# A weight ring laid out in steps of 32 bytes beside the activations: one core, a two-layer decoder trunk

## The chip, the core and the metric

The kernel runs on one core of a Trainium2 chip. The metric is device time in microseconds (us) of one execution. The kernel before takes 1014.76 us (median of 3 runs, 1014.67 to 1014.93). The profile shown here was taken of the run of 1014.67 us; its instructions span 1012.9 us, and the remaining 1.8 us lie before the first and behind the last of them.

The engines are named as the profile names them: PE (TensorE, matmul), PEld (its weight loads, which run beside the matmuls), DVE (VectorE), ACT (ScalarE), POOL (GpSimd), SP (SyncE, which issues the DMAs).

## What is computed

The reference is a trunk of two layers on 256 rows of 1024 numbers. Each layer is a SwiGLU block, a token mixer and a second SwiGLU block, each with RMSNorm before and behind it:

```python
def swiglu(h, w_gate, w_up, w_down):
    return (jax.nn.silu(h @ w_gate) * (h @ w_up)) @ w_down

for layer in range(DEPTH):
    g = norm_gains[layer]
    h = rmsnorm(x, g[0])
    x = x + 0.5 * rmsnorm(swiglu(h, w_ffn_gate[layer, 0], w_ffn_up[layer, 0], w_ffn_down[layer, 0]), g[1])
    h = rmsnorm(x, g[2])
    x = x + rmsnorm(token_mixer(h, w_in[layer], w_out[layer], ...), g[3])
    h = rmsnorm(x, g[4])
    x = x + 0.5 * rmsnorm(swiglu(h, w_ffn_gate[layer, 1], ...), g[5])
```

Everything is float32. The hidden width of a SwiGLU block is 2816 and the mixer's input projection is 3072 wide, so nearly all the arithmetic is dense products of 256 rows with 1024-deep weights.

## The kernel before

**Three matmuls per product.** A float32 operand is split into a high part (rounded to fp32r) and a low part (the rest). `mm3` forms one product as high by high, high by low and low by high, so each 128-deep step of a product is three matmuls, each with its own weight load of 128 columns.

**The weight ring.** All weights pass through `half`: SP issues a DMA of 512 KB into one of 5 `raw` buffers, ACT copies it to the high part of a ring buffer (line 271), and DVE writes the low part (line 274). There are 10 ring buffers, `ring0` to `ring9`, each of two parts (high and low) of 1024 floats per partition. PE reads them from there, and a buffer is given back when its last matmul is through.

**The activations.** `xt` (two parts, 8 x 256 floats) holds the normed input of the current block, transposed. The 12 `h` buffers (512 floats) hold, in pairs of high and low, the hidden rows of a SwiGLU block, the mixed heads of the mixer, and its values.

**Which operand moves.** A matmul loads one operand (128 columns, the weight load) and streams the other (the moving operand). The program has three large kinds, all recorded at line 362, and the profile names them with the moving operand first:
- `xt,ring`, 256 columns, 4320 of them: the ring is loaded, `xt` moves. These are the gate and up products (`gb`) and the mixer's queries and keys (`qk`). In `gb`, 96 matmuls follow one another and use four ring buffers, 24 each; a gate or up tile lies in two buffers, and PE changes between them every 12 matmuls.
- `ring,xt`, 256 columns, 1056: `xt` is loaded and the ring moves. These are the first gate and up tiles of each block (`ga`) and the mixer's values (`vstep`).
- `ring,h`, 512 columns, 1248: `h` is loaded and the ring moves. These are the down products (`down`, 24 or 12 in a row, two ring buffers) and the mixer's output.

**Order.** `Program.run` plans all operations at build time, by their listed durations, and writes each engine's instructions in that order. The plan does not know where a buffer lies.

**Where the buffers lie.** `Slots.take` makes the tile of a slot when the slot is first used, and the pool lays the tiles one behind the other in that order, each rounded up to 32 bytes. So the place of a buffer modulo 256 bytes follows from the small tiles that happened to be made before it. In the built program `xt` (both parts), `ring0` and `ring1` lie at 96 modulo 256, `ring2` to `ring9` and `h1` to `h11` at 160, and `h0` at 32. The two parts of a ring buffer lie at the same place modulo 256. All slices that matmuls read begin at multiples of 512 bytes within their buffers, so the place modulo 256 of an operand is that of its buffer.

Of the kernel before, what the change touches and what calls it, by code (L numbers as in the profile page):

```python
# [8 lines left out]
F32 = mybir.dt.float32  # L9
# [5 lines left out]
SEQ, D, FF, DEPTH = 256, 1024, 2816, 2  # L15
KC = D // 128
# [14 lines left out]
RING = 10  # L31
# [34 lines left out]
    return c  # L66


class Slots:


    def __init__(self, pool, tag, n, shape, parts=1):
        self.pool, self.tag, self.shape, self.parts = pool, tag, shape, parts
        self.idle = list(range(n))
        self.n = 0

    def take(self, dtype):
        i = self.idle.pop(0)
        self.n += 1
        t = [self.pool.tile(self.shape, dtype, tag=f"{self.tag}{i}_{p}", name=f"{self.tag}{i}_{p}_{self.n}") for p in range(self.parts)]  # L80
        return i, (t[0] if self.parts == 1 else t)


# [15 lines left out]
class Program:  # L99
# [7 lines left out]
    def op(self, eng, dur, fn, after=(), bufs=(), spare=None, lag=None):  # L107
        o = Op()
        o.eng, o.dur, o.fn, o.after, o.bufs = eng, dur, fn, [a for a in after if a is not None], list(bufs)
        o.spare, o.lag, o.idx = spare or {}, lag, len(self.ops)  # L110
        for b in o.bufs:
            b.left += 1
        self.ops.append(o)
        return o
# [99 lines left out]
def act_us(n, psum, extra=0):  # L214
    return (0.05 if psum else 0.092) + 0.000833 * n + 0.093 * extra
# [6 lines left out]
def trunk(tc, x, norm_gains, w_gate, w_up, w_down, w_in, w_out, dlam, subln, consts, out):  # L222
    nc = tc.nc
    ctx = ExitStack()
    P1 = ctx.enter_context(tc.tile_pool(name="one", bufs=1))
# [3 lines left out]
    G = Program()  # L229
    op = G.op  # L230
    PS = Slots(PSM, "ps", 8, [128, 512])
    RAW = Slots(P1, "raw", NRAW, [128, 1024])
    RNG = Slots(P1, "ring", RING, [128, 1024], 2)
    XTS = Slots(P1, "xt", 1, [128, KC, SEQ], 2)
    H2 = Slots(P1, "h2", 12, [128, 512])
    ES = Slots(P1, "e", N_ES, [128, 512])
    PT = Slots(P1, "pt", N_PT, [128, 512])
    SN = Slots(P1, "sn", N_SN, [128, 384])
# [18 lines left out]
    def half(pieces, cut=2):  # L257

        h = Half()
        raw, h.ring = Buf(RAW), Buf(RNG, F32R)  # L260

# [76 lines left out]
    def warm():  # L338

        z, p = Buf(H2, BF16), Buf(PS)  # L340
        o = op("POOL", 0.2, lambda: nc.gpsimd.memset(z.t, 0.0), [], [z])
# [19 lines left out]
    def mm(o, a, b, start=False, stop=False):  # L361
        nc.tensor.matmul(o, a, b, start=start, stop=stop, skip_group_check=True)  # L362
# [12 lines left out]
    def first_gain(i):  # L375

        p = Buf(PS)
        o = op("PE", 1.0, lambda: mm(p.t, ones, grow[:, HALF[i]], True, True), [o_row, o_small], [p])
# [79 lines left out]
    class XT:  # L458


        def __init__(self):
            self.b = Buf(XTS, F32R)
            self.done = [None, None]
# [7 lines left out]
    def turn(T, xt, hs):  # L471
        xt.done[T] = []
        for b in range(2):
            h, oh = hs[b]
            p = Buf(PS)

# [23 lines left out]
    def rows_op(p, c0, xt, T, hs, first):  # L500

        o = None
        for kh in range(2):
            def pe(kh=kh):
                for k in range(4 * kh, 4 * kh + 4):
                    wh, wl = wk(hs, k)
                    mm3(p.t[:, c0:c0 + 256], xt.hi(k, TS(T)), xt.lo(k, TS(T)), wh, wl, first and k == 0, k == KC - 1)
            o = op("PE", 1.31, pe, [xt.done[T][kh], o] + hs[kh].ready, [p, xt.b, hs[kh].ring])
        return o


    def ffn(l, s, xt, na, turn1, g, final, nxt, pre):
# [4 lines left out]
        def tile_(kind, j):  # L517
            if (kind, j) not in tiles:
                if kind == "D":
                    tiles[kind, j] = [half_row(wd, 256 * j + 128 * c) for c in range(2)]  # L520
                else:
                    tiles[kind, j] = half_cols(wg if kind == "G" else wu, 256 * j)
            return tiles[kind, j]
# [3 lines left out]
        def hbuf(j):  # L527
            if j not in hb:
                hb[j] = (Buf(H2, F32R), Buf(H2, F32R))
            return hb[j]  # L530
# [4 lines left out]
        def ga(j, T):  # L535
            pg, pu, sg = Buf(PS), Buf(PS), Buf(ES)
            og = rows_op(pg, 0, xt, T, tile_("G", j), True)
            a = op("ACT", act_us(256, True), lambda: nc.scalar.activation(sg.t[:, :256], pg.t[:, :256], AF.Silu), [og], [pg, sg])
            ou = rows_op(pu, 0, xt, T, tile_("U", j), True)
            m = op("DVE", dve_us(256), lambda: nc.vector.tensor_tensor(sg.t[:, 256:], pu.t[:, :256], sg.t[:, :256], OP.mult), [ou, a], [pu, sg])  # L540
            rows[j, T] = (sg, m)

        def hturn(j, T):
            sg, m = rows[j, T]
            p = Buf(PS)
            bh, bl = hbuf(j)
# [14 lines left out]
        def gb(j):  # L561
# [3 lines left out]
            for part in range(2):  # L565
                p = Buf(PS)
                hs = tile_("GU"[part], j)
# [75 lines left out]
    def mixer(l, xt, turn1, g, nxt, o_cst, o_misc):  # L643
# [5 lines left out]
        def vstep(T, t):  # L649
            if vt[t] is None:  # L650
                vt[t] = half_v(wi, t)
            if t % 2 == 0:
                V[T, t // 2] = (Buf(PS), Buf(H2), [])
            p, v, os = V[T, t // 2]
# [128 lines left out]
        def put_mixed(i, src, after, buf):  # L783
            t = Buf(H2, F32R)
            o1 = op("ACT", act_us(256, True), lambda: nc.scalar.activation(t.t[:, 0:256], src(), AF.Copy), after, [buf, t])
            o2 = op("DVE", dve_us(256), lambda: nc.vector.tensor_tensor(t.t[:, 256:512], src(), t.t[:, 0:256].bitcast(F32), OP.subtract), [o1], [buf, t])
            mixed[i] = (t, o2)
# [186 lines left out]
    xt = XT()  # L974
# [99 lines left out]
```

## Time and profile before

| | before |
|---|---|
| median of 3 runs | 1014.76 us |
| profiled execution | 1014.67 us, span 1012.9 us |
| granted TensorE clock, mean | 0.998 of 2.4 GHz |
| PE busy | 997.9 us, 99% |
| PEld busy | 923.8 us, 91% |
| DVE busy | 632.1 us, 62% |
| ACT busy | 582.3 us, 57% |
| DMA | 182.86 MB, mean 181 GB/s |

A matmul's row shows the length of one instruction from its start to its modelled end, 276 to 283 ns for 256 columns, and the matmuls overlap in the pipeline. What a matmul costs in a dense run is the distance from one start to the next, here called its **pace**. It is read from a row of the timeline that merges n matmuls: the row's length less the length of one, divided by n - 1; or from two such rows that follow one another without a gap, as the difference of their starts divided by n.

### The profile page before, as it was taken

To read this page: it belongs to the slowest core of one execution; us is meant where nothing else is said; L and a number is where in the kernel's file an instruction comes from. 1 tells how busy PE (TensorE), PEld (TensorE's weight loads), DVE (VectorE), ACT (ScalarE), POOL (GpSimd) and SP (SyncE) were. 2 spreads that over 40 slices of the span, in tenths; PEclk is the share of its full clock that TensorE was granted. 3 is DMA by queue.
4 is the path that set the end of the run, shared out by engine and by line. 5 is a ranking of instruction groups with operands and counts; after the bars stand their busy time and mean duration, and the time that the engine had idled before them with its cause. 6 is when DMAs were issued, how large, how long until landed. Compare 5 with 4: busy or idle time off the path is not lost.

```text
span 1012.9 us, 18113 instructions
## 1 busy us (share of the span) xinstructions
PE 997.9 (99%) x7144; PEld 923.8 (91%) x7144; DVE 632.1 (62%) x1123; ACT 582.3 (57%) x1133; POOL 34.1 (3%) x59
## 2 busy tenths in 40 slices
PE   8999999999999999999999999999999999999997
PEld 6999999898888999999899999999998789999996
DVE  6755544778897745454685454448799776545433
ACT  6654443769996544443665444447899765444431
POOL 1000000100002000000000000002000020000000
PEclk9999999999999999999999999999999999999999
DMA  8986664684345766654577666557732547666531
GB/s 267 328 268 190 186 178 142 199 247 111 108 119 179 238 189 186 193 181 152 168 230 225 193 184 201 148 164 227 213 105 85 160 152 234 186 194 181 165 104 42
DMA packets 157432, 182.86 MB, mean 181 GB/s; under 512 B 6049, under 2 KB 141473, under 8 KB 157218
## 3 DMA queue, kind: packets, MB, share of 16 engines
q1 hardware_dynamic: 157202, 181.43, 59.5%
q8 instruction: 56, 0.92, 0.4%
q10 hardware_dynamic: 144, 0.26, 0.1%
q14 instruction: 30, 0.25, 0.1%
HBM read 180.62 MB, written 1.05 MB: 179 GB/s over the span
## 4 chain that ended last, share of the span: by engine, by line
PE 87%; ACT 8%; DVE 2%; issue 1%; DMA 1%; POOL 0%; DVEq 0%; POOLq 0%; SPq 0%; ACTq 0%
PE ps L362 85%; ACT q L696 2%; ACT ring L271 1%; ACT q L712 1%; PE ps L479 1%; ACT e L763 1%; DMA raw<-in_w_in 1%; ACT junk L405 0%; DVE q L700 0%; ACT sn L841 0%; ACT sn L842 0%; DVE ring L274 0%; DMA grow<-in_norm_gains 0%; ACT sn L840 0%; POOL sm L415 0%
## 5 line engine op out<-in xcount | busy, mean ns | idle before, releaser
L271 ACT ACTIVATE ring<-raw 128x512 fp32r<-128x512 f32 (+1 forms) x552 | 367.8, 706 | 324.5 <-issue 228.2
L274 DVE TENSOR_TENSOR ring<-raw,ring 128x512 fp32r<-128x512 f32 (+1 forms) x552 | 414.8, 788 | 201.3 <-ACT ring L271 196.9
L362 PE MATMUL ps<-xt,ring 128*128 128x256 f32 x4320 | 519.2, 281 | 0.0
L362 PEld LDWEIGHTS ps<-xt,ring 128*128 128x128 f32 x4320 | 513.0, 189 | 4.8 <-issue 1.7
L362 PE MATMUL ps<-ring,h 128*128 128x512 f32 x1248 | 297.6, 393 | 0.0
L362 PEld LDWEIGHTS ps<-ring,h 128*128 128x128 f32 x1248 | 230.0, 188 | 47.4 <-issue 0.3
L362 PE MATMUL ps<-ring,xt 128*128 128x256 f32 x1056 | 130.3, 282 | 1.5 <-DVE xt L485 1.5
L362 PEld LDWEIGHTS ps<-ring,xt 128*128 128x128 f32 x1056 | 127.0, 189 | 2.8 <-DVE xt L485 2.1
L581 DVE TENSOR_TENSOR e<-ps,e 128x512 f32<-128x512 f32 x37 | 25.6, 692 | 111.0 <-PE ps L362 111.0
L414 POOL TENSOR_SCALAR sm<-sm 128x1 f32<-128x1 f32 x24 | 15.9, 661 | 928.0 <-ACT junk L405 715.3
L582 ACT ACTIVATE h<-e 128x512 fp32r<-128x512 f32 x37 | 23.2, 627 | 25.4 <-DVE e L581 25.4
L430 DVE TENSOR_TENSOR e<-ps,gpo 128x512 f32<-128x512 f32 x24 | 16.4, 689 | 21.2 <-ACT junk L405 20.8
L405 ACT ACTIVATE junk<-ps 128x512 bf16<-128x512 f32 x24 | 14.3, 596 | 26.4 <-PE ps L362 25.4
L362 PE MATMUL ps<-q,q 128*128 128x256 f32 (+3 forms) x128 | 25.9, 295 | 3.3 <-DVE q L701 2.3
L712 ACT ACTIVATE q<-ps 64x256 fp32r<-64x256 f32 x72 | 27.1, 376 | 0.8
L579 ACT ACTIVATE e<-ps 128x512 f32<-128x512 f32 x37 | 21.9, 592 | 9.8 <-PE ps L362 9.8
L362 PEld LDWEIGHTS ps<-q,q 128*128 128x128 f32 (+1 forms) x128 | 19.3, 187 | 8.7 <-issue 1.8
L583 DVE TENSOR_TENSOR h<-e,h 128x512 fp32r<-128x512 f32 x37 | 25.4, 687 | 0.0
L763 ACT ACTIVATE e<-sn,sm 128x256 f32<-128x256 f32 (+1 forms) x56 | 24.7, 446 | 0.1
L696 ACT ACTIVATE q<-ps 32x256 fp32r<-32x256 f32 x64 | 23.9, 374 | 0.9
L716 DVE SCALAR_TENSOR_TENSOR q<-ps,q 64x256 fp32r<-64x256 f32 x48 | 20.2, 421 | 1.0
L482 ACT ACTIVATE xt<-ps 128x512 fp32r<-128x512 f32 x24 | 13.2, 590 | 11.2 <-PE ps L479 11.1
(86 smaller groups left out, 396.9 us busy)
## 6 DMA issues: line engine op xcount, KB each, us to landing
raw<-in_w_ffn_gate SPq DMA_DIRECT2D x88, 512.0 KB, 4.5
raw<-in_w_ffn_up SPq DMA_DIRECT2D x88, 512.0 KB, 4.8
raw<-in_w_ffn_down SPq DMA_DIRECT2D x88, 512.0 KB, 4.3
raw<-in_w_in SPq DMA_DIRECT2D x40, 512.0 KB, 5.3
raw<-in_w_out SPq DMA_DIRECT2D x16, 512.0 KB, 3.6
raw<-in_w_in SPq DMA_DIRECT2D x16, 256.0 KB, 4.1
gpo<-in_norm_gains SPq DMA_DIRECT2D x6, 512.0 KB, 6.1
gpr<-in_norm_gains SPq DMA_DIRECT2D x5, 512.0 KB, 5.6
```

The lines of the kernel that those rows point to most:

```text
L271: nc.scalar.activation(h.ring.t[0][:, s], raw.t[:, s], AF.Copy)
L274: nc.vector.tensor_tensor(h.ring.t[1][:, s], raw.t[:, s], h.ring.t[0][:, s].bitcast(F32), OP.subtract)
L362: nc.tensor.matmul(o, a, b, start=start, stop=stop, skip_group_check=True)
L430: nc.vector.tensor_tensor(y.t, accs[i].t, gv(), OP.mult)
L579: a = op("ACT", act_us(512, True), lambda p=p: nc.scalar.activation(sg.t, p.t, AF.Silu), os[-1:], [p, sg])
L581: m_ = op("DVE", dve_us(512), lambda p=p: nc.vector.tensor_tensor(sg.t, p.t, sg.t, OP.mult), os[-1:] + [a], [p, sg])
L582: o1 = op("ACT", act_us(512, False), lambda: nc.scalar.activation(bh.t, sg.t, AF.Copy), [m_], [sg, bh])
L583: o2 = op("DVE", dve_us(512), lambda: nc.vector.tensor_tensor(bl.t, sg.t, bh.t.bitcast(F32), OP.subtract), [o1], [sg, bh, bl])
L696: nc.scalar.activation(b.t[QB[e], :], p.t[QB[m], :256], AF.Copy, scale=scale)
L712: nc.scalar.activation(bs[b].t[HB[b ^ e], :], p.t[HB[b], :256], AF.Copy, scale=scale)
L716: nc.vector.scalar_tensor_tensor(lo[b].t[HB[b ^ other], :], p.t[HB[b], :256], scale, bs[b].t[HB[b], :].bitcast(F32), OP.mult, OP.subtract)
L763: nc.scalar.activation(e.t[:, SEG[a]], sn.t[:, SEG[a]], AF.Exp, bias=mn.t[:, a:a + 1], scale=-1.0, accum_out=den.t[:, d0 + a:d0 + a + 1])
```

## The change

No instruction is added, removed or moved: the instructions of every engine, their operands, waits and order are those of before. Only places in SBUF differ. `Slots` can now make all its tiles at once (`pads`), with a row that is longer than what is used (`extra`). `xt` and `h` are made first, then the ring, then all else as before:

```diff
+BASE_PAD = 16
 class Slots:
-    def __init__(self, pool, tag, n, shape, parts=1):
+    def __init__(self, pool, tag, n, shape, parts=1, pads=None):
...
+        self.extra = 0
+        if pads is not None:
+            self.extra = pads[0]
+            for p in range(parts):
+                for i in range(n):
+                    self.one(i, p, F32)
+                if pads[1]:
+                    pool.tile([128, pads[1]], F32, name=f"{tag}pad{p}")
...
+    P1.tile([128, BASE_PAD], F32, name="basepad")
+    XTS = Slots(P1, "xt", 1, [128, KC, SEQ], 2, (0, 0))
+    H2 = Slots(P1, "h2", 12, [128, 512], 1, (0, 0))
+    RNG = Slots(P1, "ring", RING, [128, 1024], 2, (8, 48))
     RAW = Slots(P1, "raw", NRAW, [128, 1024])
-    RNG = Slots(P1, "ring", RING, [128, 1024], 2)
-    XTS = Slots(P1, "xt", 1, [128, KC, SEQ], 2)
-    H2 = Slots(P1, "h2", 12, [128, 512])
```

A ring row is now 1032 floats, 4128 bytes, which is 32 more than a multiple of 256. The 48 floats behind each part bring the second part back to the places of the first. In the built program `xt` and all `h` buffers lie at 192 modulo 256, and buffer i of the ring at 192 + 32 i modulo 256, both parts alike. `raw` moves from 32 to 160 modulo 256 to 96 to 224, and the other buffers move too.

Below, the **distance** of a matmul is the place of its ring buffer less the place of the activation buffer it is multiplied with, modulo 256. Counted in the two built programs:

| distance | `xt,ring` before | after | `ring,xt` before | after | `ring,h` before | after |
|---|---|---|---|---|---|---|
| 0 | 768 | 888 | 288 | 240 | 972 | 240 |
| 32 | | 888 | | 240 | | 240 |
| 64 | 3552 | 384 | 768 | 144 | 8 | 108 |
| 96 | | 384 | | 144 | | 108 |
| 128 | | 360 | | 72 | 60 | 144 |
| 160 | | 360 | | 72 | | 144 |
| 192 | | 528 | | 72 | 208 | 132 |
| 224 | | 528 | | 72 | | 132 |

## Rows read from the trace of the kernel before

**Rows 1.** The page: busy time by engine, granted clock, chain of waits.
```profile
PE 997.9 (99%) x7144; PEld 923.8 (91%) x7144; DVE 632.1 (62%) x1123; ACT 582.3 (57%) x1133; POOL 34.1 (3%) x59
...
PEclk9999999999999999999999999999999999999999
...
PE 87%; ACT 8%; DVE 2%; issue 1%; DMA 1%; POOL 0%; DVEq 0%; POOLq 0%; SPq 0%; ACTq 0%
```

**Rows 2.** The page's groups: form, count | busy us, mean ns | idle before.
```profile
L362 PE MATMUL ps<-xt,ring 128*128 128x256 f32 x4320 | 519.2, 281 | 0.0
L362 PEld LDWEIGHTS ps<-xt,ring 128*128 128x128 f32 x4320 | 513.0, 189 | 4.8 <-issue 1.7
L362 PE MATMUL ps<-ring,h 128*128 128x512 f32 x1248 | 297.6, 393 | 0.0
...
L362 PE MATMUL ps<-ring,xt 128*128 128x256 f32 x1056 | 130.3, 282 | 1.5 <-DVE xt L485 1.5
```

**Rows 3.** Waits of PE (us, times, longest), the longest of all.
```profile
PE ps L362 <- DVE q L701: 2.3, 7, 0.4
PE ps L362 <- DVE xt L485: 1.5, 2, 0.8
```

**Rows 4.** Timeline of PE, 36.9 to 200 us: start, length, group.
```profile
54.01 5.65 PE L362 MATMUL ps<-ring,h 128*128 128x512 f32 x24
59.50 11.47 PE L362 MATMUL ps<-xt,ring 128*128 128x256 f32 x96
70.81 5.76 PE L362 MATMUL ps<-ring,h 128*128 128x512 f32 x24
76.41 11.05 PE L362 MATMUL ps<-xt,ring 128*128 128x256 f32 x96
87.30 5.62 PE L362 MATMUL ps<-ring,h 128*128 128x512 f32 x24
92.75 11.57 PE L362 MATMUL ps<-xt,ring 128*128 128x256 f32 x96
104.16 5.65 PE L362 MATMUL ps<-ring,h 128*128 128x512 f32 x24
...
151.97 2.96 PE L362 MATMUL ps<-ring,h 128*128 128x512 f32 x12
154.77 11.05 PE L362 MATMUL ps<-xt,ring 128*128 128x256 f32 x96
```

**Rows 5.** Timeline of PE, 43.3 to 48.2 us: ring0 and ring1, distance 0.
```profile
43.08 5.32 PE L362 MATMUL ps<-xt,ring 128*128 128x256 f32 x43
```

**Rows 6.** Timeline of PE, 87.9 to 92.6 us: ring6 and ring7, distance 0.
```profile
87.53 5.38 PE L362 MATMUL ps<-ring,h 128*128 128x512 f32 x23
```

**Rows 7.** Timelines of PE: 215.3 to 217.5 (distance 0), 710 to 717.7, 343 to 346 us (64).
```profile
215.04 2.68 PE L362 MATMUL ps<-ring,xt 128*128 128x256 f32 x21
...
709.78 8.17 PE L362 MATMUL ps<-ring,xt 128*128 128x256 f32 x68
...
342.79 3.45 PE L362 MATMUL ps<-ring,xt 128*128 128x256 f32 x29
```

**Rows 8.** The page's groups of ACT and DVE that fill the ring.
```profile
L271 ACT ACTIVATE ring<-raw 128x512 fp32r<-128x512 f32 (+1 forms) x552 | 367.8, 706 | 324.5 <-issue 228.2
L274 DVE TENSOR_TENSOR ring<-raw,ring 128x512 fp32r<-128x512 f32 (+1 forms) x552 | 414.8, 788 | 201.3 <-ACT ring L271 196.9
```

More of the change, by code (lines that the diff above doesn't have):

```diff
@@ L75, in __init__, with one @@
         self.n = 0
+        self.extra = 0
[6 more added lines that the diff above has]
+                    pool.tile([128, pads[1]], F32, name=f"{tag}pad{p}")
+    def one(self, i, p, dtype):
+        shape = self.shape if not self.extra else [self.shape[0], self.shape[1] + self.extra]
+        t = self.pool.tile(shape, dtype, tag=f"{self.tag}{i}_{p}", name=f"{self.tag}{i}_{p}_{self.n}")
+        return t if not self.extra else t[:, 0:self.shape[1]]
     def take(self, dtype):
@@ L79, in take @@
         self.n += 1
-        t = [self.pool.tile(self.shape, dtype, tag=f"{self.tag}{i}_{p}", name=f"{self.tag}{i}_{p}_{self.n}") for p in range(self.parts)]
+        t = [self.one(i, p, dtype) for p in range(self.parts)]
         return i, (t[0] if self.parts == 1 else t)
```

## The prediction

> **What bounds the kernel now.** I read the page first. PE is busy for 99% of the span at the full granted clock and makes up 87% of the chain that ended last [rows 1]. The list of waits says that PE waits for nobody: its two longest entries sum to 3.8 us [rows 3]. ACT and DVE, which fill the ring, have 324 and 201 us idle before their ring instructions [rows 8]. So the time is the sum of the matmuls' paces, and three kinds of matmul, 6624 in number, carry it [rows 2]. The change can only act by making a matmul's pace depend on where its two operands lie.
>
> The trace can say whether it does, because the layout before is not uniform: two ring buffers of ten lie 64 bytes from the other eight, modulo 256. So I read the timeline of PE next, in stretches that use known buffers.
> - `xt,ring` at distance 0: (5.32 - 0.28) / 42 = 120.0 ns [rows 5]. At distance 64 there are two paces, for the same instruction at the same clock: from 59.50 to 70.81 us 96 matmuls take 11.31 us, 117.8 ns each, and from 76.41 to 87.30 us 96 take 10.89 us, 113.4 ns each [rows 4]. The pace doesn't drift within such a group, it holds one value or the other. Groups of 11.57 us are half at distance 0 and half at 64, at 117.8 ns. Of all 38 groups of 96 in the trace, 8 have 11.05 us, 17 have 11.47 and 13 have 11.57.
> - `ring,xt`: (2.68 - 0.28) / 20 = 120.0 ns at distance 0; (8.17 - 0.28) / 67 = 117.8 ns and (3.45 - 0.28) / 28 = 113.2 ns at distance 64 [rows 7]. The fast pace stands for one run of 36 of the 768 there, about 5%, so their mean is 117.6 ns.
> - `ring,h`: at distance 0 it settles at (5.38 - 0.39) / 22 = 226.8 ns [rows 6], but a group often needs eight or nine matmuls to settle: 54.01 to 59.50 us is 5.49 us for 24, 228.8 ns [rows 4]. I take 227.8 ns. At distance 192 it is 5.60 us for 24, 233.3 ns from 70.81 us on [rows 4].
>
> So place matters, by up to 6.6 ns a matmul, and in opposite directions: distance 0 is the slowest that is seen for 256 columns and the fastest for 512. The other observation that I use is what precedes the fast pace. The down groups at distance 192 (5.73 to 5.76 us for 24, 2.96 us for 12) are seven ahead of a group of 96, and all seven groups of 96 behind them are fast ones (two of the seven are shown) [rows 4]. Of the other 31 groups of 96 one is fast. Which pace is held seems to be decided by the timing with which a group starts, and the slow downs start it well.
>
> The Trainium skill speaks against any of this. "TensorE: Matmul & The Clock Gate", section "Step-by-step: what each phase is for", says that PE has two independent read ports into SBUF and that loading the next weights takes no read bandwidth from the running matmul. By that rule places are indifferent, and the change is worth nothing. The rows disagree, with 120.0, 117.8 and 113.4 ns for one instruction.
>
> **The change part by part.** The order of all instructions stays, so there is no wait to add or remove; what changes is the count of matmuls at each distance, as tabled with the change. The sum stands against the profiled execution, 1014.67 us, which is 0.09 us below the median.
>
> *`xt,ring`, 4320.* At distance 0 there will be 888 instead of 768: 120 x (120.0 - 116.7) = +0.4 us, where 116.7 ns is the mean of those at other distances now. That mean is from the groups: 8 x 96 = 768 matmuls fast, 17 x 96 + 13 x 48 = 2256 slow, so 25% fast, 0.25 x 113.4 + 0.75 x 117.8 = 116.7 ns. The 3432 at other distances are the largest term. Only 384 of them stand at 64, and 2520 at distances that the trace doesn't show with `xt,ring` (32, 96 to 160 and 224; 192 is 64 the other way round, which `ring,xt` shows). Their bounds are the nearest rows: 113.4 below and 120.0 above. I take the two paces of distance 64, and a larger share of the fast one. After the change 1008 of the 1248 down matmuls are off distance 0 instead of 276, so about 80% of the groups of 96 would start behind a slow one. But a group now changes its distance at every buffer, and a change of distance can lose the pace: in the 13 mixed groups the half at 64 was slow each time. I let a third be lost: 0.8 x 2/3 gives 55% fast, 115.4 ns. That is 3432 x -1.3 = -4.5 us.
>
> *`ring,xt`, 1056.* 48 fewer at distance 0 (-0.1 us). Of the 816 others I let 30% be fast instead of 5%: 0.3 x 113.2 + 0.7 x 117.8 = 116.4 against 117.6 ns, -0.9 us.
>
> *`ring,h`, 1248.* Now 972 at 227.8, 208 at 233.3 and 68 at other distances, taken at 231: mean 228.9 ns. After: 240 at 227.8, 132 at 233.3 and 876 at distances with few rows or none, between 226.8 and 233.3. I take 231, as the one distance off 0 with whole groups lies at the upper end. Mean 230.6 ns, so 1248 x 1.7 = +2.1 us.
>
> *The rest.* `raw`, `q`, `e` and the constants move too. PE reads those in some 500 short matmuls, and they keep nearly all their distances among themselves. ACT and DVE write the ring at new places: 706 and 788 ns an instruction [rows 8]. Were these longer by a tenth, 37 and 41 us of work would fall into idle time of 324 and 201 us. I put nothing for either.
>
> The sum: +0.4 - 4.5 - 1.0 + 2.1 = -3.0 us, so 1011.7 us. With every bound at its lower end (all 256-column matmuls off distance 0 at 113.3 ns, unseen downs at 226.8) it is about -16 us, 998. With every bound at its upper end (2520 and 672 at 120.0, the known ones all slow, downs off 0 at 233.3) it is about +15 us, 1030.
>
> **The rivals.**
> *The fast pace gets lost (slower).* PE meets a new distance every 12 matmuls in a gate or up tile, and none of the 13 mixed groups, which change theirs once, holds 113.4 in either half. If no group holds 113.4 any more, the 3432 go from 116.7 to 117.8, +3.8 us, and with the downs' +2.1 and the +0.3 of the rest that is 1020.9 us; with the unseen distances nearer to 120 it goes on to 1030. For it: 117.8 and 120.0 are what a group holds behind a quick down, and distances never seen may be as bad as 0. Against it: the entry behind slow downs was fast seven times of seven. It decides below a fast share of some 21%, where the sum reaches +2.0 us; at about 35% the sum is zero.
> *No change.* The terms have both signs, and at a fast share of 21% to 48% they cancel to within 2.0 us, which is 0.2%, about what a measurement of this kernel can tell from no change. Time 1014.7 us. The skill's rule above gives the same by another way; the rows speak against that way, not against the result.
> *Nearly all fast.* If distances off 0 are all good once the start is good, the lower bound is near: -11.3 + 0.4 - 3.7 + 2.1 = -12.5 us with the downs as forecast, 1002 us. Against it, distance 64 alone has 75% slow now.
> That the change doesn't do what it says is no rival: the built program has the ring in steps of 32 as described.
>
> **How the numbers follow.** Forecast 1011.7 us, 36%; nearly all fast, 9%; no change, 20%; slower, 35%. Faster by over 0.2% is the first two, 45%; the likeliest case's own range is 1003 to 1012.6 us. Since both signs hold much, the range that should hold the time 8 times in 10 reaches from 1003 to 1024 us: below it lies most of the nearly-all-fast case, above it the upper third of the slower one, together less than 2 in 10.
>
> **What would show it.** The timeline of PE after, by group. The first step is right if groups of 96 show paces by buffer, and more of them at 113 than 8 of 38. The second is right if the down groups of 24, now 5.60 to 5.76 us, stand mostly at 5.7. If groups of 96 are all 11.4 us or more, the slower case holds. If a pace shows that lies under 113 or well over 120, my bounds were wrong. If paces are as before at each distance but the time differs, something other than PE has moved.

## The result and the profile after

The changed kernel takes 1022.42 us (median of 4 runs, 1022.33 to 1022.54), against 1014.85 us for the kernel before beside it. That is a ratio of 1.0073, with a 95% interval of 1.0055 to 1.0090: slower by 7.6 us, where 3 us faster was forecast. The time lies inside the range, on the other side of zero.

The page of the changed kernel, which answers to [rows 1], [rows 2] and [rows 8] (all lines stand 18 further down than before: L362 is now L380, L271 is L289, L274 is L292):

```profile
PE 1005.5 (99%) x7144; PEld 928.3 (91%) x7144; DVE 632.4 (62%) x1123; ACT 583.0 (57%) x1133; POOL 34.1 (3%) x59
...
PEclk9999999999999999999999999999999999999999
...
PE 85%; ACT 9%; DVE 2%; issue 2%; DMA 1%; POOL 0%; DVEq 0%; POOLq 0%; SPq 0%; ACTq 0%
...
L289 ACT ACTIVATE ring<-raw 128x512 fp32r<-128x512 f32 (+1 forms) x552 | 367.8, 705 | 329.1 <-issue 231.5
L292 DVE TENSOR_TENSOR ring<-raw,ring 128x512 fp32r<-128x512 f32 (+1 forms) x552 | 414.5, 787 | 206.0 <-ACT ring L289 200.5
L380 PE MATMUL ps<-xt,ring 128*128 128x256 f32 x4320 | 524.2, 281 | 0.0
...
L380 PE MATMUL ps<-ring,h 128*128 128x512 f32 x1248 | 301.3, 396 | 0.0
...
L380 PE MATMUL ps<-ring,xt 128*128 128x256 f32 x1056 | 130.0, 282 | 1.7 <-DVE xt L503 1.7
```

The reader should see three things. PE's busy time rose by 7.6 us (997.9 to 1005.5), which is the whole loss. PE still waits for next to nothing: the idle time before the three large kinds is 1.7 us in all, and the granted clock is the same (0.998 before, 0.999 here). ACT and DVE fill the ring as fast as before (705 and 787 ns, where it was 706 and 788) and have a little more idle time, since the kernel is longer. So the loss lies in the paces of the matmuls, as the prediction said any effect would have to.

PE's timeline of the changed kernel, in the stretch of [rows 4]: start and length in us, then the group.

```profile
54.50 5.73 PE L380 MATMUL ps<-ring,h 128*128 128x512 f32 x24
60.07 11.40 PE L380 MATMUL ps<-xt,ring 128*128 128x256 f32 x96
71.31 5.74 PE L380 MATMUL ps<-ring,h 128*128 128x512 f32 x24
76.89 11.51 PE L380 MATMUL ps<-xt,ring 128*128 128x256 f32 x96
88.23 5.74 PE L380 MATMUL ps<-ring,h 128*128 128x512 f32 x24
93.81 11.60 PE L380 MATMUL ps<-xt,ring 128*128 128x256 f32 x96
...
156.05 11.31 PE L380 MATMUL ps<-xt,ring 128*128 128x256 f32 x96
```

The down groups of 24, 5.60 to 5.76 us before, now take 5.72 to 5.77. The groups of 96 went from three lengths (11.05, 11.47, 11.57 us) to a spread from 11.31 to 11.60 us. The eight groups of 11.05 us, at 113.4 ns a matmul, are gone.

A group of 96 now crosses buffers at different distances, so I paired the matmuls in program order with the starts in the trace. The difference of two starts is the pace of the first, and its ring buffer gives its distance. The sums by kind of neighbouring pair, before and after, add up to the loss: between two `xt,ring` matmuls +5.0 us, between two `ring,h` +3.6, between two `ring,xt` -0.1, at the borders of these groups +0.2, between the short matmuls of the other stages -0.9. Together that is +7.7 us, which is the difference of the spans (1012.9 and 1020.6 us). The mean paces by distance, in ns, are these; differences over 280 ns (20 of `ring,h` and 3 to 5 of `ring,xt` in each kernel) count in the sums but not in the means:

| distance | `xt,ring` before | after | `ring,h` before | after | `ring,xt` after |
|---|---|---|---|---|---|
| 0 | 120.5 | 120.3 | 228.2 | 231.2 | 121.7 |
| 32 | | 118.9 | | 233.0 | 119.7 |
| 64 | 117.0 | 116.6 | | 230.0 | 118.6 |
| 96 | | 119.8 | | 234.5 | 121.5 |
| 128 | | 119.1 | 233.1 | 232.3 | 118.1 |
| 160 | | 120.1 | | 233.5 | 119.2 |
| 192 | | 117.1 | 233.1 | 232.6 | 116.9 |
| 224 | | 117.7 | | 232.2 | 118.1 |
| all | 117.6 | 118.8 | 229.3 | 232.3 | 119.8 |

The same can be seen in rows of the timeline, cut inside one group. Each row is the 12 matmuls of one ring buffer (13 where the last one before it is also in the cut). From the top: distance 32; 64; 96; the buffer at 64 again; 160; 64 and 96 in a later group.

```profile
44.58 1.58 PE L380 MATMUL ps<-xt,ring 128*128 128x256 f32 x12
...
76.89 1.58 PE L380 MATMUL ps<-xt,ring 128*128 128x256 f32 x12
...
78.18 1.69 PE L380 MATMUL ps<-xt,ring 128*128 128x256 f32 x13
...
79.71 1.53 PE L380 MATMUL ps<-xt,ring 128*128 128x256 f32 x12
...
83.83 1.72 PE L380 MATMUL ps<-xt,ring 128*128 128x256 f32 x13
...
158.87 1.53 PE L380 MATMUL ps<-xt,ring 128*128 128x256 f32 x12
...
160.12 1.72 PE L380 MATMUL ps<-xt,ring 128*128 128x256 f32 x13
```

Worked out as in the prediction: (1.58 - 0.28) / 11 = 118.2 ns at 32; at 64 also 118.2 and behind it (1.69 - 0.28) / 12 = 117.5 at 96; 120.0 at 160. At 79.71 us the buffer at 64 that was slow before the one at 96 is fast behind it, (1.53 - 0.28) / 11 = 113.6 ns: the pace turned within the group. In the last two rows distance 64 holds this fast pace, and the buffer at 96 behind it pays for that with 120.0. This pair is the heart of the result, and the section on the reasons comes back to it.

### The profile page after: what moved, and what is told of

The parts are those of the page before. It is cut to its first block, busy times and chain, and to the rows that moved or that the text cites. A ratio compares the mean times of both kernels' runs of the same rounds, so it can differ in the third digit from the quotient of the medians.

```text
span 1020.6 us, 18113 instructions
## 1 busy us (share of the span) xinstructions
PE 1005.5 (99%) x7144; PEld 928.3 (91%) x7144; DVE 632.4 (62%) x1123; ACT 583.0 (57%) x1133; POOL 34.1 (3%) x59
## 4 chain that ended last, share of the span: by engine, by line
PE 85%; ACT 9%; DVE 2%; issue 2%; DMA 1%; POOL 0%; DVEq 0%; POOLq 0%; SPq 0%; ACTq 0%
PE ps L380 83%; ACT q L714 2%; ACT ring L289 2%; ACT q L730 1%; DMA raw<-in_w_in 1%; ACT e L781 1%; PE ps L497 1%; DVE ring L292 1%; ACT junk L423 0%; ACT sn L859 0%; ACT sn L860 0%; DMA grow<-in_norm_gains 0%; ACT sn L858 0%; POOL sm L433 0%; DVE q L734 0%
## 5 line engine op out<-in xcount | busy, mean ns | idle before, releaser
L289 ACT ACTIVATE ring<-raw 128x512 fp32r<-128x512 f32 (+1 forms) x552 | 367.8, 705 | 329.1 <-issue 231.5
L292 DVE TENSOR_TENSOR ring<-raw,ring 128x512 fp32r<-128x512 f32 (+1 forms) x552 | 414.5, 787 | 206.0 <-ACT ring L289 200.5
L380 PE MATMUL ps<-xt,ring 128*128 128x256 f32 x4320 | 524.2, 281 | 0.0
L380 PEld LDWEIGHTS ps<-xt,ring 128*128 128x128 f32 x4320 | 517.8, 189 | 5.1 <-issue 1.7
L380 PE MATMUL ps<-ring,h 128*128 128x512 f32 x1248 | 301.3, 396 | 0.0
L380 PEld LDWEIGHTS ps<-ring,h 128*128 128x128 f32 x1248 | 230.1, 188 | 50.7 <-issue 0.3
L380 PE MATMUL ps<-ring,xt 128*128 128x256 f32 x1056 | 130.0, 282 | 1.7 <-DVE xt L503 1.7
L380 PEld LDWEIGHTS ps<-ring,xt 128*128 128x128 f32 x1056 | 126.7, 189 | 3.0 <-DVE xt L503 2.3
L380 PE MATMUL ps<-q,q 128*128 128x256 f32 (+3 forms) x128 | 25.8, 294 | 3.1 <-DVE q L719 2.0
L380 PEld LDWEIGHTS ps<-q,q 128*128 128x128 f32 (+1 forms) x128 | 19.4, 187 | 8.3 <-issue 1.5
```

The costliest lines, as they stand in the source:

```text
L289: nc.scalar.activation(h.ring.t[0][:, s], raw.t[:, s], AF.Copy)
L292: nc.vector.tensor_tensor(h.ring.t[1][:, s], raw.t[:, s], h.ring.t[0][:, s].bitcast(F32), OP.subtract)
```

## The experiments

Questions after the result: does each distance have a pace of its own, or does the changing of distance cost? Is it the distance that counts, or the places themselves? And what lets a group hold 113.4 ns? In the expectations, the theory that the timing of a group's start decides (slow downs bring the fast pace) is the entry theory, A; that each distance has its own price is C; that every change of distance costs is D. All kernels have the instructions of before and after, word for word and in the same order; only places differ. The paces that follow are worked out from a group's length as above, with 0.28 us for the last matmul of 256 columns and 0.39 for one of 512.

Most kernels use one edit of the changed kernel. It lays `xt`, the `h` buffers and the ring at chosen places modulo 256, with unused gaps between them (the matmuls' line is then L388):

```diff
+class Place:
+    def __init__(self, pool, start):
+        self.pool, self.at, self.n = pool, start, 0
+    def to(self, r):
+        gap = (r - self.at) % 256
+        if gap:
+            self.n += 1
+            self.pool.tile([128, gap // 4], F32, name=f"gap{self.n}")
+            self.at += gap
...
-    XTS = Slots(P1, "xt", 1, [128, KC, SEQ], 2, (0, 0))
-    H2 = Slots(P1, "h2", 12, [128, 512], 1, (0, 0))
-    RNG = Slots(P1, "ring", RING, [128, 1024], 2, (8, 48))
+    place = Place(P1, 1152)
+    XTS = Slots(P1, "xt", 1, [128, KC, SEQ], 2, place, [XT_AT])
+    H2 = Slots(P1, "h2", 12, [128, 512], 1, place, [H_AT] * 12)
+    RNG = Slots(P1, "ring", RING, [128, 1024], 2, place, RING_AT)
```

The kernels differ in three numbers, and the ratio is to the kernel before:

| kernel | ring less `xt` | ring less `h` | us | ratio, 95% interval |
|---|---|---|---|---|
| u64_h0 | 64 | 0 | 1014.05 | 0.9988 [0.9977, 0.9999] |
| u64_h192 | 64 | 192 | 1012.39 | 0.9974 [0.9960, 0.9988] |
| u160 | 160 | 160 | 1030.76 | 1.0149 [1.0120, 1.0179] |
| u0 | 0 | 0 | 1025.49 | 1.0097 [1.0068, 1.0127] |
| shift32 | as changed | as changed | 1022.23 | 1.0074 [1.0044, 1.0103] |
| u32 | 32 | 32 | 1022.24 | 1.0074 [1.0044, 1.0103] |
| u224 | 224 | 224 | 1017.79 | 1.0029 [1.0017, 1.0041] |
| s64 | 0, 64, 128, 192 in turn | the same | 1021.90 | 1.0073 [1.0050, 1.0096] |
| u192_h0 | 192 | 0 | 1013.43 | 0.9986 [0.9975, 0.9998] |
| s128 | 64 and 192 in turn | 0 and 128 in turn | **1000.80** | 0.9862 [0.9834, 0.9891] |
| s128_h64 | 64 and 192 in turn | 192 and 64 in turn | 1006.07 | 0.9915 [0.9887, 0.9944] |

### Does each distance have a price of its own? u160 and u0

u160 puts all at distance 160, the worst in the table that before never shows. It never changes distance. u0 takes the step of 32 out of the changed kernel: every ring buffer at distance 0.

```diff
+XT_AT = 192
+H_AT = 192
+RING_AT = [96, 96, 96, 96, 96, 96, 96, 96, 96, 96]
```

> All ring buffers at distance 160 from xt and h, so the distance never changes. Theory C (each distance has its own pace, and 160 is a bad one): groups of 96 at 120.0 ns (11.68 us), downs at 233 to 234 ns, time about 1029 us. Rival D (160 is as good as 64, and it was the change of distance from buffer to buffer that cost): groups of 96 at 113.4 or 117.8 ns, time 1008 to 1017 us.

```diff
+XT_AT = 192
+H_AT = 192
+RING_AT = [192, 192, 192, 192, 192, 192, 192, 192, 192, 192]
```

> The layout of after with the step between ring buffers taken out: xt, h and all ring buffers at the same place modulo 256, distance 0 throughout. Theory C: groups of 96 all at 120.0 ns (11.68 us), downs at 227 to 228 ns, ring,xt at 120 ns: 4320 x +2.9, 1056 x +0.5 and 1248 x -1.5 ns make about 1026 us. Rival D (steadiness is what counts): 1015 us or less.

PE's timeline, u160 first, then u0:

```profile
43.34 11.68 PE L388 MATMUL ps<-xt,ring 128*128 128x256 f32 x96
54.86 5.77 PE L388 MATMUL ps<-ring,h 128*128 128x512 f32 x24
```

```profile
43.46 11.68 PE L388 MATMUL ps<-xt,ring 128*128 128x256 f32 x96
54.98 5.63 PE L388 MATMUL ps<-ring,h 128*128 128x512 f32 x24
```

Both have all 38 groups at 11.67 or 11.68 us, 120.0 ns a matmul. u160 is the slowest kernel of all, and neither of the two changes its distance anywhere. So each distance has a price of its own, and D falls as the main cause. Of the three large kinds the two kernels differ in the downs alone, 5.77 against 5.63 us for 24, (5.77 - 5.63) / 23 = 6.1 ns each and some 7.6 us over 1248. The times differ by 5.3 us. Paired start to start, the downs differ by 6.9 us and `xt,ring` by 0.2, while `ring,xt`, the borders of the groups and the short matmuls each give some 0.6 us back.

### The distance, or the places? shift32

All buffers lie 32 bytes further than in the changed kernel, so every distance stays.

```diff
-BASE_PAD = 16
+BASE_PAD = 24
```

> The changed kernel with all its buffers 32 bytes further on: xt and h at 224 modulo 256, every distance as in after. Theory C (only the distance of the two operands counts): paces by buffer as in after, time 1022.4 us within 1 us. Rival E (the place itself modulo 256 counts, and distance only looked like it): other paces by buffer, a time off by several us.

It takes 1022.23 us, 0.2 us from the changed kernel, and the mean pace of `xt,ring` is 118.8 ns in both. Distance 64 also has the same two paces in the kernel before, with `xt` at 96, and in u64_h192 below, with `xt` at 192. Nor do multiples of 256 bytes matter: in s64 below, the high parts of `ring0`, `ring4` and `ring8` lie 0, 256 and 512 bytes from that of `xt` modulo 1024, and 90 of their 92 buffers of 12 matmuls settle at 120.0 ns. So what counts is the difference of the two places modulo 256.

### Two distances by themselves: u32 and u224

32 and 224 are the same step to either side.

```diff
+RING_AT = [224, 224, 224, 224, 224, 224, 224, 224, 224, 224]
```

> All ring buffers at distance 32 from xt and h. Theory C: the paces that the two ring buffers at 32 show in after, 118.9 ns for xt,ring, 117.6 for ring,xt and 233.4 for ring,h, so about 1025 us. Rival D: 1017 us or less.

```diff
+RING_AT = [160, 160, 160, 160, 160, 160, 160, 160, 160, 160]
```

> All ring buffers at distance 224 from xt and h. Theory C: the paces of the buffer at 224 in after, 116.0 to 118.0 ns for xt,ring (117.1 mean), 231.4 for ring,h, so 1014 to 1018 us. Were 32 and 224 alike, as a distance counted without its direction would have it, it would be u32's time, about 1025 us.

The timeline, u32 first, then u224:

```profile
42.89 11.52 PE L388 MATMUL ps<-xt,ring 128*128 128x256 f32 x96
54.25 5.76 PE L388 MATMUL ps<-ring,h 128*128 128x512 f32 x24
```

```profile
43.01 11.36 PE L388 MATMUL ps<-xt,ring 128*128 128x256 f32 x96
54.21 5.76 PE L388 MATMUL ps<-ring,h 128*128 128x512 f32 x24
```

That is 118.3 ns at 32 and 116.6 at 224. u224 came out as expected, u32 some 3 us below. Direction matters: it isn't only how near the two operands lie. No group of either is at 113.4 ns.

### What finds the fast pace? u64_h0, u64_h192 and u192_h0

All `xt,ring` stand at 64, behind quick downs (distance 0) in the first kernel and behind slow ones (192) in the second. By A the second has all its groups at 11.05 us.

```diff
+XT_AT = 192
+H_AT = 0
+RING_AT = [0, 0, 0, 0, 0, 0, 0, 0, 0, 0]
```

> All ten ring buffers at distance 64 from xt and at distance 0 from every h buffer; no instruction differs. Theory A (a group of 96 xt,ring matmuls is fast only behind a slow down group, and here no down is slow): hardly any group of 11.05 us, nearly all 11.47, downs at about 227.5 ns, time 1012 to 1014 us. Rival B (the fast pace comes by chance or from elsewhere, a quarter of the groups as before): 10 or so groups of 11.05 us, time about 1009 us.

```diff
+XT_AT = 192
+H_AT = 64
+RING_AT = [0, 0, 0, 0, 0, 0, 0, 0, 0, 0]
```

> All ring buffers at distance 64 from xt and 192 from h. Theory A: every down group is slow (5.76 us for 24), so nearly every group of 96 is fast (11.05 us, 113.4 ns); 4320 x -3.6 ns and 1248 x +4 ns make about 1004 us. Rival B: a quarter of the groups fast, as before, so only the slower downs are left: 1016 to 1018 us.

```profile
42.93 11.47 PE L388 MATMUL ps<-xt,ring 128*128 128x256 f32 x96
54.23 5.60 PE L388 MATMUL ps<-ring,h 128*128 128x512 f32 x24
59.67 11.47 PE L388 MATMUL ps<-xt,ring 128*128 128x256 f32 x96
```

```profile
43.16 11.05 PE L388 MATMUL ps<-xt,ring 128*128 128x256 f32 x96
54.05 5.75 PE L388 MATMUL ps<-ring,h 128*128 128x512 f32 x24
59.64 11.47 PE L388 MATMUL ps<-xt,ring 128*128 128x256 f32 x96
70.95 5.76 PE L388 MATMUL ps<-ring,h 128*128 128x512 f32 x24
76.55 11.06 PE L388 MATMUL ps<-xt,ring 128*128 128x256 f32 x96
```

u64_h0 (above) has 36 of its 38 groups at 11.47 us and 2 at 11.06, as A expects. u64_h192 was half a miss: its groups alternate, 20 fast and 18 slow, behind downs of the same length, and it takes 1012.4 us where A gave some 1004. So the downs do decide how a group begins, but behind a fast group the same slow downs bring a slow one. The seven cases of seven in the trace before were a sample of this, not the rule that I made of it.

u192_h0 asks whether 192 finds the fast pace better than 64 does.

```diff
+XT_AT = 192
+H_AT = 128
+RING_AT = [128, 128, 128, 128, 128, 128, 128, 128, 128, 128]
```

> All ring buffers at distance 192 from xt and 0 from h. It tells why the alternating ring held 113.3 ns. If distance 192 finds the fast pace by itself: nearly all groups of 96 of 11.05 us, downs at 227 ns, about 998 us. If it is the change between 64 and 192 that finds it: groups of 11.47 us behind the quick downs as in the uniform kernel at 64, about 1014 us.

```profile
42.52 11.47 PE L388 MATMUL ps<-xt,ring 128*128 128x256 f32 x96
53.83 5.64 PE L388 MATMUL ps<-ring,h 128*128 128x512 f32 x24
```

It doesn't: all 38 groups take 11.47 us, and the kernel is like u64_h0.

### Distances in turn: s128, s128_h64 and s64

s128 has ring buffers at 64 and 192 in turn for `xt`, and 0 and 128 for `h`. s128_h64 has the same for `xt`, with the downs at 192 and 64. s64 is the changed kernel with a step of 64 in place of 32.

```diff
+XT_AT = 192
+H_AT = 0
+RING_AT = [0, 128, 0, 128, 0, 128, 0, 128, 0, 128]
```

> Ring buffers alternate between distance 64 and 192 from xt, so the distance changes at every buffer, but only between two that were good before; from h they alternate between 0 and 128. Theory C: xt,ring stays at 117.8 or 113.4 ns; half the downs go from 227 to 232 ns, +3 us against the uniform kernel of 1014.05 us, so 1015 to 1018 us. Rival D (a change of distance at every buffer costs of itself): settled paces near 119 or 120 ns as in after, 1022 us or more.

```diff
+XT_AT = 192
+H_AT = 64
+RING_AT = [0, 128, 0, 128, 0, 128, 0, 128, 0, 128]
```

> The alternating ring (64 and 192 from xt) with h moved so that the downs stand at 192 and 64 in place of 0 and 128. If the change between 64 and 192 holds the fast pace: xt,ring at 114.5 ns again, downs at 231 to 232 ns, 1000 to 1003 us. If the downs at 0 and 128 were what started the groups well (theory A): a part of the groups back at 117.8 ns, 1005 to 1012 us.

```diff
-    RNG = Slots(P1, "ring", RING, [128, 1024], 2, (8, 48))
+    RNG = Slots(P1, "ring", RING, [128, 1024], 2, (16, 32))
```

> The change with a step of 64 bytes from one ring buffer to the next where it has 32: distances 0, 64, 128 and 192 only. Theory C (a price to each distance, taken from the runs so far: xt,ring 120.3, 116, 119 and 116 ns; ring,h 229.5, 230, 232.3 and 232.9 ns): mean 117.9 and 230.9 ns, so 1017 to 1019 us. If the odd multiples of 32 are what is dear, and all multiples of 64 but 0 are as 64 is, 128 would be at 113 to 118 ns and the time near 1014 us.

The timelines, in the order s128, s128_h64, s64:

```profile
42.36 11.04 PE L388 MATMUL ps<-xt,ring 128*128 128x256 f32 x96
53.24 5.70 PE L388 MATMUL ps<-ring,h 128*128 128x512 f32 x24
58.77 11.04 PE L388 MATMUL ps<-xt,ring 128*128 128x256 f32 x96
```

```profile
42.64 11.15 PE L388 MATMUL ps<-xt,ring 128*128 128x256 f32 x96
53.63 5.70 PE L388 MATMUL ps<-ring,h 128*128 128x512 f32 x24
```

```profile
42.86 11.50 PE L380 MATMUL ps<-xt,ring 128*128 128x256 f32 x96
54.20 5.73 PE L380 MATMUL ps<-ring,h 128*128 128x512 f32 x24
```

s128 was a miss by 14 us to the good side: 1000.8 us, faster than both kernels. 35 of its 38 groups take 11.04 us, 113.3 ns a matmul. Neither of its distances does that alone (u64_h0, u64_h192, u192_h0). Its page shows the gain where it should be: `xt,ring` is busy for 505.5 us, 13.7 us less than before [rows 2].

```profile
L388 PE MATMUL ps<-xt,ring 128*128 128x256 f32 x4320 | 505.5, 277 | 0.0
L388 PE MATMUL ps<-ring,h 128*128 128x512 f32 x1248 | 299.2, 394 | 0.0
L388 PE MATMUL ps<-ring,xt 128*128 128x256 f32 x1056 | 129.2, 282 | 1.5 <-DVE xt L511 1.5
```

s128_h64 and s64 show why, when the pace that a buffer of 12 settles at (the starts of its seventh to its twelfth matmul, paired with the program as above) is counted against that of the buffer ahead of it. "Fast" is 113.3 ns, "slow" 117.5 to 118:

| kernel | step in `xt,ring` | ahead, then | count |
|---|---|---|---|
| before | 64 to 64 | fast stays fast / slow stays slow | 56 / 152 |
| u64_h192 | 64 to 64 | fast stays fast / slow stays slow | 141 / 119 |
| s128_h64 | 192 to 64 | fast stays fast / slow **turns fast** | 74 / 36 |
| s128_h64 | 64 to 192 | fast stays fast / slow stays slow | 113 / 37 |
| s128 | both | fast stays fast / slow turns fast / slow stays slow | 257 / 1 / 2 |
| s64 | 0 to 64 | fast / slow | 17 / 68 |
| s64 | 128 to 192 | fast / slow | 0 / 65 |
| changed | 96 to 64 | fast / slow | 13 / 0 |
| changed | fast 64 to 96 | 120.0 | 16 of 16 |
| changed | slow 64 to 96 | 117.2 to 117.4 | 10 of 10 |
| changed | fast 192 to 224 | 116.4 to 116.6 | 12 of 12 |

At one distance a buffer keeps the pace that it finds; only the break between groups can change it. At the step from 192 to 64 the slow pace turned fast 37 times of 37, and a fast pace was never lost at either step. In the changed kernel the buffer at 64 was fast behind one at 96 13 times of 13. So in s128_h64 a group whose first buffer is slow is fast from the next step on (11.15 us), and in s128 the downs at 0 and 128 also start it well (11.04). In s64 the same two distances have 0 and 128 for neighbours. Behind 0 a buffer at 64 finds the fast pace 17 times of 85, behind 128 one at 192 never does: 1021.9 us, 3 to 5 above what was expected.

What makes a step turn the pace inside TensorE is not shown by any row, and stays open. So does what sets the pace of one distance; uniform 96 and 128 weren't run.

## Why the prediction was wrong

*The bound* held. PE's paces make the time, nothing waits, and a change of places alone moved it: 1000.8 to 1030.8 us over the kernels above, with one instruction stream. The Trainium skill ("TensorE: Matmul & The Clock Gate", section "Step-by-step: what each phase is for") says that loading the next weights takes no read bandwidth from the running matmul. Read as the prediction reads it, that places are indifferent, this would have had all of these kernels at 1014.7 us; the measurement decides against it here. That only the distance modulo 256 counts held too (shift32).

*The step that failed* is the price of the distances that the trace before doesn't show. I gave 2520 of the 4320 `xt,ring` matmuls "the two paces of distance 64", and a larger share of the fast one. Measured, they have paces of their own, 118.9 (32), 119.8 (96), 119.1 (128), 120.1 (160) and 117.7 ns (224), and none of these distances held 113.3 once. Together they came to 119.0 ns, 3.6 above the 115.4 that I took, which over 2520 matmuls is 9.1 us. So the term that should have been -4.5 us, with +0.4 beside it for distance 0, was +5.0. The bounds of 113.4 and 120.0 held for the means (160 went 0.1 past the upper one, and single buffers there settle at up to 121.0), but the value that I took, 115.4, lies in their lower third. The row at distance 0 [rows 5] stands as near to 32 as those at 64 [rows 4], and nearer to 224; I priced these distances by one side only.

*The entry* (slow downs start a group well), from which the fast share of 55% came, did not carry over. In the changed kernel 16 buffers at 64 or 192 stand first behind a down group, and 3 of them hold the fast pace. At distance 64 the buffers do hold it more often, 19 of 30 (63%) against 25% before, but for another reason: 13 of the 19 are those behind a buffer at 96. It isn't the slowness of the downs that starts a group well, either: s128 and s128_h64 have downs of the same 5.70 us, and the first buffer behind them is fast in 35 groups of 36 in s128 and in none of 36 in s128_h64. What u64_h0 and u64_h192 show is narrower: the places of the downs act on how the next group begins, in u64_h192 for 20 groups of 38, not all.

The fast buffers at 64 bring little. They are part of 384 matmuls of 4320, and the gain is taken back next door: the buffer at 96 behind a fast one takes 120.3 ns on average instead of 117.4. From start to start such a pair of buffers costs 117.4 ns a matmul, against 117.7 where both are slow. The prediction's "a change of distance can lose the pace" was the right doubt, let in at a third; with steps of 32 no group of the 38 kept the pace from end to end.

*The downs* had the right sign and too small a size. The term was +2.1 us; the mean pace went from 229.3 to 232.3 ns, and the sum by pairs is +3.6 us. Distances 32, 96, 160 and 224 lie at 232 to 234.5, not at 231, and distance 0 no longer settles at the 226.8 ns of [rows 6]: with a new distance every few matmuls its mean went from 228.2 to 231.2.

*`ring,xt`* should have gained 1.0 us and gained 0.1: its mean pace is 119.8 ns, where 119.5 was before. *The rest*, at nothing, was right for ACT and DVE; the short matmuls of the other stages, whose buffers moved too, gave back 0.9 us.

*The rivals.* "The fast pace gets lost" is the case that came: 1020.9 us by its working, 1022.4 measured, with the addition that it names, "unseen distances nearer to 120". Its point of decision, a fast share under 21%, was met: 30 of the 250 buffers of 12 matmuls off distance 0 hold the fast pace (12%), all of them at 64 or 192, and of the 38 groups none is at 11.05 us. "Nearly all fast" (1002 us) is what s128 reached, by another layout.

## What to carry to other kernels

When TensorE is busy all the time with weight loads and matmuls back to back, the places of the two operands modulo 256 bytes are worth 1.4% to one side and 1.5% to the other here, for no change of any instruction; keep them in view whenever buffers are moved for other reasons. Spreading buffers over many distances averages good and bad ones; measure the uniform distances one by one, then try two good ones in turn, since 64 and 192 in turn (1000.8 and 1006.1 us, by where `h` lies) beat each of them alone (1012.4 to 1014.1). A price for a case that the trace doesn't show belongs between its neighbours on both sides, not at the one that the forecast likes.

## What the runs showed of the hardware

One matmul of 128x256, at the full granted clock, settles at paces from 113.3 to 121.0 ns that depend on where its operands lie; the commonest are 113.3, 116.5, 117.8, 118.2 to 119.0 and 120.0 ns. Which one holds depends on the distance and on the buffer ahead: distance 96 takes 117.4 ns behind a slow 64 and 120.3 behind a fast one. The pace carries on from buffer to buffer for as long as 96 matmuls. Direction matters (118.3 ns at 32, 116.6 at 224). For 512 columns the order is another: of the distances that were run uniformly (0, 32, 160, 192, 224) 0 is the best (226.5 ns in u64_h0, from 5.60 us for 24) and 160 the worst (233.9 ns, from 5.77 us).
